# A decoder trunk's output projection, from one product per token tile to Strassen's seven products

## Chip, cores and metric

The kernel is one program on 1 core of a Trainium2 chip. The metric is the device time of one execution in microseconds (us). The engines are named as in the profile: PE (TensorE matmul; PEld is its weight load), DVE (VectorE), ACT (ScalarE), POOL (GpSimd) and SP (SyncE), whose queue SPq issues most DMAs.

## What is computed

One hybrid mixer layer for 2048 prompt tokens and 32 sample tokens (8 x 4). Four channel groups of 512 are made and gated, put side by side to 2048 channels, and projected to 1024 columns:

```python
mix = jnp.concatenate([y_c * jax.nn.silu(cg), y_p * jax.nn.silu(pg),
                       y_s * jax.nn.silu(sg), y_m * jax.nn.silu(mg)], axis=-1)   # conv, pool, attention, memory
out = rms_norm(mix @ w_out, post_g)       # (tokens, 2048) @ (2048, 1024)
return x + out, ...                       # then a final rms_norm over 1024 columns
```

Everything is float32. The change concerns `mix @ w_out` and the work that runs beside it.

## The kernel before

The program has three parts in time. First, up to about 1500 us, the input projection `z` on PE, with the sample group's attention over gathered pages (POOL issues the gathers), the depthwise convolution on DVE and the memory attention woven in. Then the prompt's stick-breaking attention, up to about 1979 us. Last the output projection, with the rest of the conv branch (`conv_post`) woven in. Every finished quarter of `mix` lies in DRAM as `mixd[16, 128, tokens]`: 16 chunks of 128 channels, group g being chunks 4g to 4g+3 (0 conv, 1 pool, 2 attention, 3 memory).

PE's order is the order of the code; the other engines' orders are set by a scheduler when the kernel is built, and each engine then works strictly in that order. `sp.dma_start` and `wq.dma_start` both go to SP's queue, which is in order too. A tile taken from a pool with `bufs=n` waits until the tile n places earlier is no longer read.

A float32 product is made of three matmuls on reduced operands: hi x hi, hi x lo, lo x hi, where hi is a cast to `fp32r` (ACT) and lo the difference (DVE). For the projection, `out_weights` loads a 128 x 512 piece of `w_out` (`wor`) and splits it into `wohi` and `wolo`. `out_mix` loads a part, that is 128 tokens of one group (`mr`, 256 KB in runs of 512 B), and splits it into `mh` (ACT) and `ml` (DVE). `out_part` makes a part's matmuls into the PSUM tile `acc`: 4 channel chunks x 3, each 128 x 512. A token tile has 4 parts in each column half; 16 prompt tiles and a tile of the 32 sample tokens (2 matmuls per chunk) give 1600 matmuls. `order` lists (column half, token tile, group): in half 0 the conv group is taken `LAG` = 5 tiles late, since `conv_post` still makes it. `out_keep` copies half 0 to SBUF, and `out_tile` does both norms and the residual once half 1 is there. `prepare` splits `AHEAD` = 4 parts ahead of PE.

`conv_post` has eight blocks of 256 tokens (the last 288). For each: `cs`, the sum over four channel chunks of `cy`; its mean by a matmul `cm`; centring of `cy`; squares `csq` and their sum; a variance by a matmul `cv`; root and reciprocal `crs`; scale, sigmoid `csg` and split into `shi` and `slo`; then four pointwise products `cz` of 12 matmuls each. Each `cz` is multiplied with a gate loaded into `cgt` and stored to `mixd`. `cgt` has two buffers, which `cs` uses too. `OPACE` sets how many PE steps lie between two steps of `conv_post`.

## Time and profile before

| | us |
|---|---|
| three runs | 2425.78, 2427.82 (median), 2430.87 |
| profiled execution, its own time | 2425.78 |
| its span from first to last instruction | 2424.1 |
| PE, DVE, ACT, POOL busy | 2321.3, 1633.9, 1108.1, 1235.3 |

The profiled execution is the fastest of the three, 2.0 us under the median. Busy times of PE overlap, because a matmul's record lasts longer than the step to the next one; how densely PE works is read from the starts of its matmuls.

### The profile page before, as it was taken

Reading aid. Unit: us, or ns where it says so; the run is one execution under the profiler, and the core shown is the slowest. Engines: PE = TensorE matmul, PEld = TensorE weight load, DVE = VectorE, ACT = ScalarE, POOL = GpSimd, SP = SyncE. Lnnn points to the kernel's source line nnn. Section 1 sums busy time; section 2 is a strip of 40 time slices with the busy share of each in tenths; the row PEclk is TensorE's granted clock in tenths of the full one; section 3 lists DMA queues with packets and bytes.
Section 4 is the critical chain, followed back from the end, with each engine's and each line's share of the span. In section 5 each row is a group of like instructions: output and inputs, shape, how many; then the busy total and the mean of one; then the engine's idle time right before and its main releaser. Section 6 shows DMA issues by size and latency. Waiting matters only on the chain. (4 is left out here: it accounts for less than half of the span.)

```text
span 2424.1 us, 42161 instructions
## 1 busy us (share of the span) xinstructions
PE 2321.3 (96%) x16154; PEld 1806.4 (75%) x16154; DVE 1633.9 (67%) x2268; ACT 1108.1 (46%) x1890; POOL 1235.3 (51%) x1289
## 2 busy tenths in 40 slices
PE   6999999999999899999999998999999989999998
PEld 6998878898888677777777776555555558788786
DVE  5332775959747663577877778788898846565554
ACT  5332353242442222223241434788988955444443
POOL 1554545556474555555556564667776833320222
PEclk9999999999999999999999999999999999999999
DMA  5688988878778899877778767733323125446564
GB/s 184 206 265 293 346 315 288 283 260 281 250 262 302 271 344 326 315 267 274 275 266 275 259 222 188 215 77 112 94 79 92 36 88 146 130 117 190 164 203 132
DMA packets 350931, 526.47 MB, mean 217 GB/s; under 512 B 27585, under 2 KB 252225, under 8 KB 334330
## 3 DMA queue, kind: packets, MB, share of 16 engines
q1 hardware_dynamic: 295354, 255.07, 34.8%
q0 software_dynamic: 55376, 268.72, 31.2%
q8 instruction: 127, 2.08, 0.3%
q14 instruction: 74, 0.61, 0.1%
HBM read 448.31 MB, written 76.00 MB: 216 GB/s over the span
## 5 line engine op out<-in xcount | busy, mean ns | idle before, releaser
L903 DVE STREAM_TRANSPOSE T<-kt 128x1024 f32<-128x1024 f32 x256 | 308.9, 1226 | 192.5 <-PE sSA L916 174.4
L870 POOL DMA_INDIRECT vt<-in_cache_v_dram,idv x256 | 250.7, 979 | 240.4 <-PE sO L955 179.3
L561 DVE SCALAR_TENSOR_TENSOR cacc<-U,par,cacc 128x512 f32<-128x512 f32 x480 | 360.3, 751 | 11.8
L1255 POOL TENSOR_TENSOR be<-be,E 128x512 f32<-128x512 f32 (+2 forms) x320 | 303.3, 955 | 116.9 <-DVE E L1246 50.8
L1246 DVE TENSOR_TENSOR_SCAN E<-gam,cr,ZM 128x513 f32<-128x513 f32 x192 | 233.2, 1265 | 15.6 <-ACT gam L1231 13.7
L870 POOL DMA_INDIRECT kt<-in_cache_k_dram,idk x128 | 125.9, 983 | 204.2 <-DVE T L903 150.3
L1649 PE MATMUL acc<-wohi,mh 128*128 128x512 f32 (+1 forms) x544 | 219.6, 404 | 3.9 <-ACT mh L1479 3.9
L1649 PE MATMUL acc<-wolo,mh 128*128 128x512 f32 (+1 forms) x544 | 213.7, 393 | 0.0
L1266 PEld LDWEIGHTS AT<-ident,be 128*128 128x128 f32 x1088 | 117.8, 142 | 127.7 <-ACT at L1272 44.0
L1649 PE MATMUL acc<-wohi,ml 128*128 128x512 f32 x512 | 202.5, 396 | 1.1 <-DVE ml L1482 1.1
L1231 ACT ACTIVATE gam<-S,nbias_bc 128x1024 f32<-128x1024 f32 (+1 forms) x160 | 172.3, 1077 | 51.5 <-ACT be L1233 19.5
L1226 PE MATMUL S<-kT,Q 128*128 128x512 f32 (+1 forms) x640 | 177.9, 401 | 6.8 <-DMA Q<-qd 2.8
L1266 PE MATMUL AT<-ident,be 128*128 128x128 f32 x1088 | 158.4, 284 | 14.2 <-DVE at L1270 3.9
L1233 ACT ACTIVATE be<-S,bias_bc 128x1024 f32<-128x1024 f32 (+1 forms) x160 | 171.2, 1070 | 0.0
L1282 PE MATMUL av<-at,V 128*64 128x512 f32 (+3 forms) x640 | 153.0, 557 | 1.8 <-DVE sbo L1287 1.8
L916 PE MATMUL sSA<-T,W 128*32 128x128 f32 x4096 | 139.9, 277 | 4.3 <-DVE T L903 3.5
L1479 ACT CAST mh<-mr 128x512 fp32r<-128x512 f32 (+1 forms) x136 | 79.3, 600 | 127.5 <-PE acc L1649 71.0
L916 PEld LDWEIGHTS sSA<-T,W 128*32 128x32 f32 x4096 | 105.0, 110 | 41.8 <-issue 35.5
L1510 POOL TENSOR_TENSOR oxt<-oxt,oy 128x1024 f32<-128x1024 f32 (+1 forms) x16 | 43.6, 2724 | 179.5 <-DVE oy L1505 133.6
L1482 DVE TENSOR_TENSOR ml<-mr,mh 128x512 fp32r<-128x512 f32 x124 | 97.2, 803 | 44.2 <-ACT mh L1479 43.6
L1226 PEld LDWEIGHTS S<-kT,Q 128*128 128x128 f32 x640 | 107.2, 196 | 23.0 <-issue 3.5
L955 PE MATMUL sO<-vt,saT 128*32 128x512 f32 x1024 | 122.4, 592 | 0.0
(561 smaller groups left out, 5959.4 us busy)
## 6 DMA issues: line engine op xcount, KB each, us to landing
mr<-mixd SPq DMA_DIRECT2D x128, 256.0 KB
Q<-qd SPq DMA_DIRECT2D x64, 256.0 KB
xtp<-in_x_prompt_dram SPq DMA_DIRECT2D x16, 512.0 KB
kT<-kd SPq DMA_DIRECT2D x64, 128.0 KB
wor<-in_w_out_dram SPq DMA_DIRECT2D x32, 256.0 KB
oxt<-in_x_prompt_dram SPq DMA_DIRECT2D x16, 512.0 KB
out_dram<-oy SPq DMA_DIRECT2D x15, 512.0 KB
wr0mem<-in_w_mem_kv_dram SPq DMA_DIRECT2D x8, 512.0 KB
```

Source lines behind the costliest of these rows:

```text
L561: dve.scalar_tensor_tensor(out=ps, in0=U[:, a + k : a + k + H], scalar=wd[:, k : k + 1], in1=ps, op0=ALU.mult, op1=ALU.add)
L870: pool.indirect_dma_start(out=dst, out_offset=None, in_=rows, in_offset=bass.IndirectOffsetOnAxis(ap=idx, axis=0))
L903: dve.transpose(T[:, 2 * hh : 2 * hh + 2].rearrange("p s j t -> p (s j t)"), kt[:, 2 * hh : 2 * hh + 2].rearrange("p s j d -> p (s j d)"))
L916: pe.matmul(sSs[n][32 * g : 32 * g + 32, P * ml : P * (ml + 1)], lhsT=W[:, jj, :], rhs=T[:, :, jj, :], start=i == 0, stop=i == 3, tile_pos ...
L1226: pe.matmul(S[:, j, :w], lhsT=Q[hh][:, x, P * (q2 + j) : P * (q2 + j + 1)], rhs=KT[hp, hh, kc][:, :w], start=x == 0, stop=x == 1)
L1231: act.activation(out=ga[:, :, 512 - w : 512], in_=S[:, :, :w], func=AF.Sigmoid, bias=nbias_bc[:, h : h + 1], scale=-1.0)
L1233: act.activation(out=be[:, :, :w], in_=S[:, :, :w], func=AF.Sigmoid, bias=bias_bc[:, h : h + 1])
L1246: dve.tensor_tensor_scan(out=E[:, j][:, ::-1], data0=ga[:, j][:, ::-1], data1=ZM[:, 0:1].to_broadcast([P, 513]), initial=carry[hh, q2][:, ...
L1255: pool.tensor_tensor(out=be[:, j, :m], in0=be[:, j, :m], in1=E[:, j, 513 - w : 513 - w + m], op=ALU.mult)
L1266: pe.transpose(ap_[:, P * qt : P * (qt + 1)], A[hp, qb, kc, hh, qt][:, P * r : P * (r + 1)], ident)
L1282: pe.matmul(av[64 * hh : 64 * hh + 64, c], lhsT=V[:, 4 * kc + r, 64 * hh : 64 * hh + 64], rhs=ats.pop((hp, qb, kc, r, hh))[:, c], start=dg ...
L1649: pe.matmul(o[:rows], lhsT=m[i][:, k, :rows], rhs=W[hf, 4 * g + k][w], start=g == 2 and k == i == w == 0, stop=g == 0 and k == 3 and (i if ...
```

## The change

The 2048 channels are cut into A-columns 1 (groups 2 and 3) and 2 (groups 1 and 0), the tokens into pairs of tiles (i = 0 to 7), and the columns into halves of 512. For each pair the four products of a 2 x 2 block product, eight half-size ones, are replaced with seven (Winograd's form of Strassen's scheme):

- products 1 to 7 of sums of A-blocks (`TERMS`) and of B-blocks (`operand`); a part is now (product, pair, channel half), and its matmuls are as before. `order` runs product 1 for all pairs, then 7, 6, 2, and then 5, 4, 3 pair by pair. The sample tokens (i = `LAST` = 8) use four products and no sums. 1408 matmuls remain.
- the sums of weight blocks are made in the first part by `out_sums`: 4 loads and 4 stores of 512 KB and 8 POOL operations for each of four calls, kept in DRAM as `wsd`. The weights are split once for each product: 56 pieces instead of 32.
- the sums of token blocks are made by `out_combine` (products 7 and 6 on DVE, 2 and 5 on POOL), one operation a part, and those of 7, 6 and 2 are stored to DRAM as `msd` and loaded again by the product that follows on them.
- the seven results are put together by `out_ready`: 8 DVE adds with a PSUM operand per pair, through SBUF arrays `C11`, `U2` and `U3`. The finished first block goes to DRAM (`c11d`) and comes back as `oh`.
- `out_tile` adds the residual in halves on DVE or POOL, and squares in halves.
- in `conv_post` the sums over four chunks, three POOL operations each, become one DVE `TENSOR_REDUCE` each; `csq` is one tile, `csg` has two buffers of its own, and `OPACE` is 0.66.
- `mh` and `ml` have 4 buffers instead of 6, `mr` 7 instead of 4.

```diff
-OPACE = 0.95
+OPACE = 0.66
-LAG = 5
+OH = 2
+OX = 3
+RAWS = 7
...
+    def out_sums(*js):
+        ws = {}
+        for j in js:
+            for n, rows in enumerate(half_rows(j)):
+                ws[j, n] = k4(f"ws{j}_{n}", [P, 2, 512], F32)
+                sp.dma_start(ws[j, n].rearrange("p a c -> p (a c)"), w_out0[rows])
+        for _ in range(5):
+            yield
+        for j in js:
+            (b11, b12), (b21, b22) = [(ws[j, n][:, 0], ws[j, n][:, 1]) for n in range(2)]
+            pool.tensor_tensor(out=b11, in0=b12, in1=b11, op=ALU.subtract)
...
+            wq.dma_start(wsd[j, 0], ws[j, 0])
...
-                sums[i] = channel_sum([ys[i][:, c, :N] for c in range(4)], *[
-                    cp.tile([P, CW], F32, tag="cgt", name=f"cs{n}{a0}", bufs=2)[:, :N] for n in range(2)])
+                sums[i] = cp.tile([P, CW], F32, tag="cgt", name=f"cs{a0}", bufs=2)[:, :N]
+                dve.tensor_reduce(out=sums[i], in_=ys[i][:, :, :N].rearrange("p c t -> p t c"), axis=AX.X, op=ALU.add)
...
-            sqs[i] = channel_sum(sq, sq[0], sq[2])
+            dve.tensor_reduce(out=sqs[i], in_=sq.rearrange("p c t -> p t c"), axis=AX.X, op=ALU.add)
...
+    TERMS = {1: ((0, 0),), 7: ((0, 0), (1, 0)), 6: ((1, 1), 0), 2: ((0, 1), 1), 5: ((1, 0), (1, 1)), 4: ((1, 1),),
+             3: (2,)}
...
+    def out_combine(x):
+        prod, i, h = x
+        if len(raws[x]) == 2:
+            a, b = raws[x]
+            o = a if prod == 5 else b
+            (pool if prod in (2, 5) else dve).tensor_tensor(out=o, in0=a, in1=b, op=ALU.add if prod == 5 else ALU.subtract)
+            if prod != 5:
+                sp.dma_start(msd[(7, 6, 2).index(prod), i, h], o)
...
+        if prod == 1:
+            act.copy(C11[:, i], o)
+        elif prod == 7:
+            dve.tensor_tensor(out=U3[:, i], in0=o, in1=C11[:, i], op=ALU.add)
+        elif prod == 6:
+            dve.tensor_tensor(out=U2[:, i], in0=o, in1=C11[:, i], op=ALU.add)
+            dve.tensor_tensor(out=U3[:, i], in0=o, in1=U3[:, i], op=ALU.add)
+        elif prod == 2:
+            dve.tensor_tensor(out=C11[:, i], in0=o, in1=C11[:, i], op=ALU.add)
+            square(C11[:, i], t, 0)
+            sp.dma_start(c11d[i], C11[:, i])
+        else:
+            if prod == 5:
+                dve.tensor_tensor(out=U2[:, i], in0=o, in1=U2[:, i], op=ALU.add)
+            dve.tensor_tensor(out=o, in0=o, in1=(U2 if prod == 3 else U3)[:, i], op=ALU.add)
+            half = 0 if prod == 4 else 1
+            square(o, t, half)
...
-        if not last:
-            pool.tensor_tensor(out=xt[:rows], in0=xt[:rows], in1=y[:rows], op=ALU.add)
+            (dve if last or n or t % 2 else pool).tensor_tensor(out=xt[:, hs], in0=xt[:, hs], in1=src, op=ALU.add)
+            act.activation(out=junk[:rows], in_=xt[:, hs], func=AF.Square, accum_out=ss[:, n + 1 : n + 2])
...
+    order = [(p, i) for p, n in ((1, 9), (7, 8), (6, 8), (2, 9)) for i in range(n)]
+    order += [(5, 0), (4, 0), (5, 1), (4, 1), (3, 0), (3, 1), (5, 8), (3, 8)]
+    order += [(p, i) for i in range(2, 8) for p in (5, 4, 3)]
```

DVE's order in the second conv block, from its first gate to the next block's centring. Names end in a number of their own; `ml0_6_1` is half 0, tile 6, group 1, and in the changed kernel `mr7_1_1_1` is product 7, pair 1, half 1, operand 1. Before:

```order
L1404 SCALAR_TENSOR_TENSOR cgt256_0_20471<-cz256_0_20473,par_113,cgt256_0_20471 128x256
L1482 TENSOR_TENSOR ml0_1_0_20517<-mr0_1_0_20518,mh0_1_0_20516 128x512
L1482 TENSOR_TENSOR ml0_6_2_20570<-mr0_6_2_20571,mh0_6_2_20569 128x512
L1404 SCALAR_TENSOR_TENSOR cgt256_1_20494<-cz256_1_20496,par_113,cgt256_1_20494 128x256
L1482 TENSOR_TENSOR ml0_6_3_20626<-mr0_6_3_20627,mh0_6_3_20625 128x512
L1489 COPY okeep_19991<-acc0_0_19840 128x512
L1404 SCALAR_TENSOR_TENSOR cgt256_2_20526<-cz256_2_20528,par_113,cgt256_2_20526 128x256
L1404 SCALAR_TENSOR_TENSOR cgt256_3_20549<-cz256_3_20551,par_113,cgt256_3_20549 128x256
L1482 TENSOR_TENSOR ml0_6_1_20661<-mr0_6_1_20662,mh0_6_1_20660 128x512
L1375 RECIPROCAL crs512_20585<-crs512_20585 128x256
L1380 SCALAR_TENSOR_TENSOR cy512_20166<-cy512_20166,par_113,crs512_20585 128x256 x4
```

The same place in the changed kernel:

```order
L1429 SCALAR_TENSOR_TENSOR cgt256_0_20515<-cz256_0_20517,par_116,cgt256_0_20515 128x256
L1531 TENSOR_TENSOR mr7_1_1_1_20697<-mr7_1_1_0_20695,mr7_1_1_1_20697 128x512
L1429 SCALAR_TENSOR_TENSOR cgt256_1_20545<-cz256_1_20547,par_116,cgt256_1_20545 128x256
L1531 TENSOR_TENSOR mr7_2_0_1_20718<-mr7_2_0_0_20716,mr7_2_0_1_20718 128x512
L1429 SCALAR_TENSOR_TENSOR cgt256_2_20568<-cz256_2_20570,par_116,cgt256_2_20568 128x256
L1546 TENSOR_TENSOR ml7_0_0_20670<-mr7_0_0_1_20535,mh7_0_0_20669 128x512
L1429 SCALAR_TENSOR_TENSOR cgt256_3_20588<-cz256_3_20590,par_116,cgt256_3_20588 128x256
L1531 TENSOR_TENSOR mr7_2_1_1_20802<-mr7_2_1_0_20800,mr7_2_1_1_20802 128x512
L1381 TENSOR_REDUCE cs768_20618<-cy768_20444 128x256
L1400 RECIPROCAL crs512_20622<-crs512_20622 128x256
L1389 TENSOR_TENSOR cy768_20444<-cy768_20444,cm768_20676 128x256
```

What moved: the token sums stand between the gates, and the channel sum `cs`, which takes a `cgt` buffer, stands in DVE's queue where POOL's queue had it.

DVE's order in the last stage, between two output tiles. Before (half 1, tiles 8 to 10):

```order
L1499 TENSOR_TENSOR oss7_23113<-oss7_23113,ssk_19992 128x1
L1501 RECIPROCAL oss7_23113<-oss7_23113 128x1
L1505 SCALAR_TENSOR_TENSOR oy7_23112<-okeep_19991,oss7_23113,gpost_22340 128x512
L1505 SCALAR_TENSOR_TENSOR oy7_23112<-acc1_7_23043,oss7_23113,gpost_22340 128x512
L1482 TENSOR_TENSOR ml1_9_1_23182<-mr1_9_1_23183,mh1_9_1_23181 128x512
L1517 RECIPROCAL oss7_23113<-oss7_23113 128x1
L1520 SCALAR_TENSOR_TENSOR oy7_23112<-oxt7_23110,oss7_23113,gfin_22341 128x1024
L1482 TENSOR_TENSOR ml1_9_0_23216<-mr1_9_0_23217,mh1_9_0_23215 128x512
```

In the changed kernel (products 5, 4 and 3 of pairs 3 to 5):

```order
L1611 SCALAR_TENSOR_TENSOR acc3_3_23420<-acc3_3_23420,oss6_23455,gpost_22708 128x512
L1586 TENSOR_TENSOR U2_20067<-acc5_4_23478,U2_20067 128x512
L1612 TENSOR_TENSOR oxt6_23453<-oxt6_23453,acc3_3_23420 128x512
L1587 TENSOR_TENSOR acc5_4_23478<-acc5_4_23478,U3_20068 128x512
L1546 TENSOR_TENSOR ml3_4_1_23539<-mr3_4_1_0_23491,mh3_4_1_23538 128x512
L1614 TENSOR_TENSOR oss6_23455<-oss6_23455 128x1
L1546 TENSOR_TENSOR ml5_5_0_23577<-mr5_5_0_0_23512,mh5_5_0_23576 128x512
L1616 RECIPROCAL oss6_23455<-oss6_23455 128x1
L1619 SCALAR_TENSOR_TENSOR oxt6_23453<-oxt6_23453,oss6_23455,gfin_22709 128x1024
L1587 TENSOR_TENSOR acc4_4_23520<-acc4_4_23520,U3_20068 128x512
```

What moved: the adds of `out_ready` and the residual adds stand between the splits that PE waits for.

SP's queue while half 1 is made before, with one output store for four loads of `mr`:

```order
L1477 DMA mr1_8_1_23094<-mixd_63 128x4x128
L1522 DMA out_0_dram<-oy5_22934 128x1024
L1495 DMA oxt7_23110<-in_x_prompt_dram 128x1024
L1477 DMA mr1_8_0_23128<-mixd_63 128x4x128
L1477 DMA mr1_9_2_23147<-mixd_63 128x4x128
L1477 DMA mr1_9_3_23165<-mixd_63 128x4x128
```

and in the middle of product 2 of the changed kernel:

```order
L1523 DMA mr2_3_1_0_22290<-mixd_63 128x4x128
L1497 DMA wor5_4_22250<-wsd_70 128x512
L1497 DMA wor5_5_22276<-wsd_70 128x512
L1517 DMA mr2_3_1_1_22292<-msd_71 128x512
L1533 DMA msd_71<-mr2_3_0_1_22257 128x512
L1583 DMA c11d_69<-C11_20074 128x512
L1523 DMA mr2_4_0_0_22325<-mixd_63 128x4x128
```

What moved: stores that wait for POOL or DVE (`msd`, `c11d`) stand ahead of loads that PE needs.

## The prediction

> **What bounds the kernel now.** I read the page's busy shares and its chain of waits first:

> ```profile
> PE 2321.3 (96%) x16154; PEld 1806.4 (75%) x16154; DVE 1633.9 (67%) x2268; ACT 1108.1 (46%) x1890; POOL 1235.3 (51%) x1289
> PE acc L1649 13%; PE cz L1401 1%; DMA mixd<-cgt 1%; PE av L1282 0%; PE AT L1266 0%; DMA cgt<-gcd 0%; POOL slo L1386 0%; PE cm L1361 0%; DVE crs L1375 0%; POOL cs L1336 0%; DVE cgt L1404 0%; POOL cs L1335 0%; DVE ml L1482 0%; SPq L1477 0%; PE S L1226 0%
> ```

> PE is the bound, and the chain that ends last runs through the projection's `acc`. Its first stage also has conv links (`cgt`, `slo`, `cm`, `crs`), so two stages must be told apart: the one with the conv blocks and the one behind it. In the chain in order of time and the instructions of `cz`, the blocks and the end stand at:

> ```profile
> L1401 PE MATMUL cz<-shi,pwhi x128: 276/282/416, 2005.0 to 2194.0; 128*128 128x256 f32 x112, 128*128 128x288 f32 x16
> 2184.70 1.59 PE cz L1401 x12
> 2194.55 219.17 PE acc L1649 x955
> ```

> The first of eight blocks starts its products at 2005.0 and the eighth at 2184.7: seven block steps take 179.7 us, 25.7 each. After 2194.55 PE runs 955 `acc` matmuls in one piece, 0.2295 us each. The rate inside a piece, from the timeline (first and last of 94 matmul starts in a row):

> ```profile
> 2299.55 0.39 PE L1649 MATMUL acc<-wohi,mh 128*128 128x512 f32 x1
> 2320.84 0.39 PE L1649 MATMUL acc<-wohi,mh 128*128 128x512 f32 x1
> 2060.28 0.28 PE L1401 MATMUL cz<-shi,pwhi 128*128 128x256 f32 x1
> 2061.59 0.28 PE L1401 MATMUL cz<-shi,pwlo 128*128 128x256 f32 x1
> 2066.71 0.67 PE L1372 MATMUL cv<-csq,ones_ln 128*128 128x256 f32 x2 [0.62 <-DVE cgt L1404]
> ```

> 21.29 us over 93 steps is 0.229 us per `acc` matmul, whatever its record's 0.39; 12 `cz` starts give 1.31 over 11, 0.119; a `cv` or `cm` takes 0.7. Busy time by stage (us, then PE, PEld, DVE, ACT, POOL, clock, DMA share, GB/s):

> ```profile
> 2005.00:2185.00 180.00, 171.28 (x882) 144.35 (x883) 108.70 (x176) 85.98 (x176) 62.40 (x71) 0.98 0.45 127
> 2185.00:2414.00 229.00, 228.71 (x1016) 184.43 (x1014) 119.35 (x205) 95.90 (x208) 43.62 (x17) 1.00 0.60 180
> ```

> DVE has 71 us to spare in the first of these, 110 in the second.

> **The change, part by part.** *Fewer matmuls.* 1600 become 1408: 192 x 0.229 = 44.0 us, the most PE alone could give. By PE's order both kernels have 114 `acc` matmuls ahead of the first block's `cz`; in the seven block steps there are 516 before and 355 now, behind them 970 and 939. So 161 matmuls (36.9 us) go from the conv stage and only 31 (7.1 us) from the long piece. In the conv stage PE now needs 355 x 0.229 + 336 x 0.119 + 13 x 0.7 = 130 us, 18.6 per block.

> *The conv stage on DVE.* These rows are the means of that stage, then those of the last stage, the PSUM-reading add (32 partitions of the same 512 columns), and the only transposed reduce over four chunks:

> ```profile
> L1482 DVE TENSOR_TENSOR ml<-mr,mh 128x512 fp32r<-128x512 f32 x47 | 42.2, 921 | 18.7 <-ACT mh L1479 18.6
> L1380 DVE SCALAR_TENSOR_TENSOR cy<-cy,par,crs 128x256 f32<-128x256 f32 (+1 forms) x28 | 15.1, 599 | 0.1
> L1384 DVE SCALAR_TENSOR_TENSOR cy<-cy,par,csg 128x256 f32<-128x256 f32 (+1 forms) x30 | 14.6, 540 | 4.9 <-ACT csg L1383 4.9
> L1375 DVE RECIPROCAL crs<-crs 128x256 f32<-128x256 f32 (+1 forms) x7 | 12.4, 1777 | 2.8 <-ACT crs L1374 2.8
> L1364 DVE TENSOR_TENSOR cy<-cy,cm 128x256 f32<-128x256 f32 (+1 forms) x27 | 10.2, 416 | 0.4 <-PE cm L1361 0.4
> L1404 DVE SCALAR_TENSOR_TENSOR cgt<-cz,par,cgt 128x256 f32<-128x256 f32 x28 | 13.5, 483 | 39.2 <-DMA cgt<-gcd 24.0 <-PE cz L1401 10.3 <-PE acc L1649 3.2
> L1463 DVE TENSOR_TENSOR wolo<-wor,wohi 128x512 fp32r<-128x512 f32 x11 | 7.4, 690 | 2.2 <-ACT wohi L1462 1.4 <-DMA mixd<-cgt 0.7
> L1482 DVE TENSOR_TENSOR ml<-mr,mh 128x512 fp32r<-128x512 f32 x55 | 39.9, 748 | 11.9 <-ACT mh L1479 11.7
> L1520 DVE SCALAR_TENSOR_TENSOR oy<-oxt,oss,gfin 128x1024 f32<-128x1024 f32 x14 | 18.0, 1285 | 1.5
> L1505 DVE SCALAR_TENSOR_TENSOR oy<-okeep,oss,gpost 128x512 f32<-128x512 f32 x15 | 11.3, 752 | 0.5
> L1517 DVE RECIPROCAL oss<-oss 128x1 f32<-128x1 f32 x14 | 2.3, 164 | 49.9 <-ACT oss L1516 49.9
> L1657 DVE TENSOR_TENSOR both<-both,acc x2: 669/672/676, 2231.2 to 2272.6; 32x512 f32<-32x512 f32 x2
> L1155 DVE TENSOR_REDUCE smR<-smOm 128x128 f32<-128x512 f32 x2 | 2.1, 1057 | 0.0
> ```

> The reduce has 128 outputs of four; the new ones have 256, so I take 2.1 us each (bounds: 1.06, the same row if its length did not count, and 2.5). DVE's order holds, in the seven block steps, 28 gates x 0.483 + 28 x 0.599 + 28 x 0.540 + 7 x 1.777 + 24 x 0.416 = 67.8 of conv as before; 12 reduces x 2.1 = 25.2, new; 28 splits x 0.75 and two small = 21.6 (0.75 as behind the conv stage, since most of POOL's sums that lengthened 0.75 to 0.92 are gone); 25 token sums x 0.75 = 18.8, new; 16 weight splits x 0.69 = 11.0; 12 PSUM adds x 0.67 = 8.1, and one both-add 0.7. Sum 153 us, 21.9 per block: more than PE's 130. So DVE, not PE, paces this stage: `ml` and the token sums that PE needs stand behind the conv work in its queue, and so each wait there counts. Before, the waits there were 24.0 us on gates from DMA, 18.6 on `mh`, 10.3 on `cz`, about 5 on `csg`. Those on `cz` and most on `mh` fall away when PE is ahead; the gates' round trip (store, then load into the same buffer) is partly covered by the token sums that now stand between; new on DVE is the wait of `cs` for a `cgt` buffer, which POOL had:

> ```profile
> POOL cs L1334 <- DMA mixd<-cgt: 53.2, 5, 12.1
> SPq L1396 <- DMA mixd<-cgt: 35.2, 19, 4.6
> ```

> Part of POOL's 53.2 was idleness anyway; on DVE it can cost 0 to 3 us a block. I take 2.0 us of waits a block in all (bounds 0.5 and 6; before it was over 7, with DVE half idle): 153 + 14 = 167 us against 179.7, so **-13 us** (bounds -37, PE's pace with the loss of before, below, and +15). The first block's start stays: DVE is idle until attention ends in both, 0 (-1 to +4).

> *Behind the conv stage.* PE gives **-7**. Against it: in the last stage a pair of tiles costs DVE 6 splits x 0.75 + 4 PSUM adds x 0.67 + 4 x 0.75 + 3 adds x 0.75 + 2 x 1.285 + 8 small x 0.16 = 16.3 us, and PE 72 x 0.229 = 16.5. The 110 us of slack are gone; a wait of half a us a pair shows, and the splits stand behind `oxt` loads and ACT's roots in the same queue: before, DVE waited 49.9 us for 14 such roots, 3.6 each, free in its slack. Where other work now stands between add and root, most of that is filled. I take +0.5 us a pair, **+4** (0 to +16).
> In product 2 each part moves `mr` and `msd` in, `msd` out, and its share of `c11d` and weights: 0.79 + 0.13 + 0.23 = 1.15 MB in 12 x 0.229 = 2.74 us.

> ```profile
> q1 hardware_dynamic: 33250, 28.79, 59.6%
> L1477 SPq DMA_DIRECT2D mr<-mixd x136: 359/377/1333, 1877.9 to 2391.0; - x136
> ```

> The first row is of 2245 to 2405 us: 28.79 MB took 59.6% of 160 us, 302 GB/s if always busy. At that rate a part needs 3.8 us, 16 parts +17; if c11d and weights can run late, 2.6, nothing. I take **+5** (0 to +17), nearer the second, since those weights are first used a product later. [...] SP issues 168 more DMAs x 0.38 us, 64 us of 460 that are mostly idle; that loads wait behind stores is in the waits above.

> *First part.* 32 POOL adds and 16.8 MB of DMA.

> ```profile
> 600.00:1500.00 900.00, 880.46 (x6859) 683.58 (x6852) 623.14 (x823) 292.51 (x526) 497.69 (x460) 1.00 0.80 273
> L676 POOL TENSOR_TENSOR U<-U,sg1cb 128x512 f32<-128x512 f32 x8 | 8.8, 1103 | 0.9 <-ACT sg1cb L674 0.8
> ```

> 32 x 1.1 = 35 us on a POOL with 400 us free, 56 us of DMA where 180 are free; both covered by `z` on PE. But POOL's page gathers queue behind adds that wait for their load, and PE waits for pages: **+2** (-1 to +8). ACT gains 24 casts and 8 copies at about 0.6, 19 us, with half its time free: 0. The tail gains a PSUM add and an output chain just ahead of it on DVE: **+1** (0 to +3).

> *Sum.* -13 - 7 + 4 + 5 + 2 + 1 = -8 on the profiled execution's 2425.8 (span 2424.1, 1.7 around it): **2418 us**, 0.4% under the median 2427.8, which is 2.0 above that execution. A difference under 0.2% (4.9 us) this kernel's measurement can't tell from none.

> **Rivals.** *DVE's queue makes the conv stage longer (slower).* Place: `cgt` and `cs` in DVE's order, each waiting for a store. It decides at (179.7 - 153) / 7 = 3.8 us of waits a block; with 6 us the stage takes 195, +15, and with the other terms +5 the time is 2446. For it: before, DVE waited over 7 us a block, and DMA was at 0.45 there where the changed kernel doubles its loads. Against: half of those waits were on PE.
> *The gain is given back behind the conv stage (no change).* DVE at 16.3 of 16.5 and DMA near its rate: both at half their upper bounds, +16 instead of +9, give 2425.
> *PE stays the bound (much faster).* If reduces and waits are short, the conv stage falls to PE's 130 plus what it lost before, 179.7 - (516 x 0.229 + 40 + 9.1) = 13, so 143, and behind it little is lost: 2425.8 - 37 - 7 + 5 = 2387. Against: DVE's 153.
> [...]
> That the change isn't made is excluded: 1408 matmuls stand in PE's order.

> **Chances and range.** Forecast, 2406 to 2422: 0.38, the reduce at its short bound within it. PE's pace, 2380 to 2405: 0.12. No change: 0.20. Slower, mostly by DVE's queue: 0.30. So faster 0.50, same 0.20, slower 0.30. The range 2393 to 2446 cuts half of PE's case and the longest waits; the likeliest case alone has 2406 to 2422.

> **What would show it.** Right: `acc` x1408; conv steps of 23 to 24.5 us with DVE over 85% busy; a long piece near 0.229 us a matmul; new reduces of 2 us. Wrong: DVE waits of over 4 us a block on `mixd<-cgt`, PE waits on `ml` of over 10 us behind the conv stage, a DMA share over 0.9 in product 2, or a first part that ends later than at 1513 us, where the first `E` starts:

> ```profile
> L1246 DVE TENSOR_TENSOR_SCAN E<-gam,cr,ZM x192: 1229/1262/1284, 1513.0 to 1954.5; 128x513 f32<-128x513 f32 x192
> ```

## The result, and the profile after

The changed kernel takes 2461.93 us in the median of 4 runs (2459.88 to 2464.02), the kernel before beside it 2429.35 (4 runs, 2425.78 to 2431.51): a ratio of 1.0136 (95% interval 1.0118 to 1.0153). It is 1.4% slower. The forecast was 2418 us, with a range of 2393 to 2446.

The page of the kernel after, its busy shares and the chain that ended last:

```profile
PE 2309.7 (94%) x15962; PEld 1785.2 (73%) x15962; DVE 1738.5 (71%) x2414; ACT 1121.9 (46%) x1939; POOL 1254.6 (51%) x1297
PE acc L1755 2%; DMA mr<-msd 1%; DVE ml L1546 1%; DMA wor<-wsd 1%; PE cz L1426 1%; DMA mixd<-cgt 1%; DMA mr<-mixd 0%; ACT junk L1613 0%; DVE oxt L1619 0%; DVE wolo L1505 0%; POOL mr L1531 0%; ACT junk L1551 0%; DMA cgt<-gcd 0%; POOL oxt L16
```

The products' matmuls have the names `acc`, at L1755 now, and there are 1408 of them. Before, they made 13% of the chain; now 2%, and loads, splits and casts stand in their place. PE is busy for only 11.6 us less, although 44 us of matmuls are gone. The stages tell why. Busy time in four windows, which end at the first scan `E`, the first `cz`, the eighth block's first `cz` and the last `acc`; the columns after the window are its length, then PE, PEld, DVE, ACT and POOL busy, PE's granted clock, DMA share and GB/s. The kernel before:

```profile
0.00:1513.00 1513.00, 1460.24 (x11692) 1207.80 (x11692) 1001.14 (x1371) 515.37 (x956) 803.07 (x773) 0.99 0.80 272
1513.00:2005.00 492.00, 461.10 (x2567) 269.86 (x2567) 399.99 (x509) 408.47 (x544) 326.20 (x430) 0.98 0.36 101
2005.00:2184.50 179.50, 170.78 (x878) 143.89 (x879) 108.20 (x176) 85.76 (x175) 61.90 (x71) 0.98 0.45 127
2184.50:2413.70 229.20, 229.20 (x1019) 184.89 (x1018) 119.85 (x205) 95.86 (x209) 44.12 (x17) 1.00 0.60 180
```

The kernel after, in the same stages:

```profile
0.00:1529.90 1529.90, 1468.41 (x11692) 1213.16 (x11692) 1005.00 (x1371) 515.91 (x956) 844.76 (x805) 0.99 0.82 280
1529.90:2013.90 484.00, 456.17 (x2566) 266.32 (x2566) 403.00 (x511) 409.59 (x549) 320.90 (x421) 0.99 0.38 104
2013.90:2191.70 177.80, 149.39 (x718) 121.08 (x718) 136.73 (x213) 81.74 (x156) 26.36 (x29) 0.90 0.67 201
2191.70:2441.30 249.60, 235.70 (x987) 184.64 (x987) 184.04 (x301) 109.81 (x265) 62.53 (x44) 0.96 0.81 252
```

Adding what follows the last `acc` (10.4 us before, 16.5 after), the 33.7 us between the two spans are: first part +16.9, attention and the lead of the projection -8.0, the seven steps of the conv stage -1.7, behind them +20.4, the tail +6.1.

The third rows are the heart of it. PE's need there fell by 37 us and the stage stayed as long. Its idle time is length minus busy time: 8.7 us before, 28.4 after. And the granted clock was 0.98 before and 0.90 after, so a tenth of 177.8, 17.8 us, was lost with PE busy. Take both away: 179.5 - 8.7 - 3.6 = 167.2 and 177.8 - 28.4 - 17.8 = 131.6. That is what the matmuls there need by the prediction's rates, 167 and 130. Nearly all of the 37 us came back: 19.7 as waits and 14.2 as slow clock.

What PE waited for in the seven steps before (us in total, times, longest):

```profile
PE cm L1361 <- POOL cs L1336: 5.8, 3, 2.5
PE cz L1401 <- ACT shi L1385: 2.3, 1, 2.3
PE cv L1372 <- DVE cgt L1404: 1.3, 2, 0.7
PE cz L1401 <- DVE cgt L1404: 0.8, 1, 0.8
PE cz L1401 <- POOL slo L1386: 0.7, 2, 0.5
```

And after:

```profile
PE cm L1386 <- DVE cs L1381: 13.5, 6, 3.4
PE cz L1426 <- POOL slo L1411: 7.9, 14, 2.4
PE cz L1426 <- ACT shi L1410: 5.7, 7, 1.8
PE cv L1397 <- DVE cgt L1429: 2.2, 2, 1.5
```

All four of the second list are links of the conv blocks: the channel sum `cs`, its mean on PE (`cm`), the variance (`cv`), root, scalings, sigmoid, the halves `shi` and `slo`, the products `cz`, the gates `cgt`, and then the next block's `cs`. Not one wait is for the projection's splits.

How a wait is paid twice, from PE's timeline after (start, duration; idle time before it in brackets):

```profile
2158.53 0.39 PE L1755 MATMUL acc<-wolo,mh 128*128 128x512 f32 x1
2158.76 0.40 PE L1755 MATMUL acc<-wohi,ml 128*128 128x512 f32 x1
2162.53 0.81 PE L1386 MATMUL cm<-cs,ones_ln 128*128 128x288 f32 x2 [3.38 <-DVE cs L1381]
2163.56 0.63 PE L1755 MATMUL acc<-wolo,mh 128*128 128x512 f32 x1
2163.99 0.63 PE L1755 MATMUL acc<-wohi,ml 128*128 128x512 f32 x1
...
2166.77 0.40 PE L1755 MATMUL acc<-wohi,mh 128*128 128x512 f32 x1
2167.00 0.39 PE L1755 MATMUL acc<-wolo,mh 128*128 128x512 f32 x1
```

Ahead of the wait of 3.38 us the starts are 0.23 us apart, behind it 0.43, and from 2166.77 on 0.23 again: for about 3.4 us PE works at half speed (the granted clock is 0.60 over the 4.3 us from 2162.5 to 2166.8, that is half for 3.4 of them).

### The profile page after: what moved, and what is told of

Same layout as the page of the kernel before. It is cut to its first block, busy times and chain, and to the rows that moved or that the text cites. A ratio compares the mean times of both kernels' runs of the same rounds, so it can differ in the third digit from the quotient of the medians.

```text
span 2457.8 us, 42287 instructions
## 1 busy us (share of the span) xinstructions
PE 2309.7 (94%) x15962; PEld 1785.2 (73%) x15962; DVE 1738.5 (71%) x2414; ACT 1121.9 (46%) x1939; POOL 1254.6 (51%) x1297
## 5 line engine op out<-in xcount | busy, mean ns | idle before, releaser
L1278 DVE TENSOR_TENSOR_SCAN E<-gam,cr,ZM 128x513 f32<-128x513 f32 x192 | 232.9, 1263 | 14.4 <-ACT gam L1263 13.1
L1755 PE MATMUL acc<-wohi,mh 128*128 128x512 f32 (+1 forms) x480 | 199.2, 415 | 8.1 <-ACT mh L1543 8.0
L1263 ACT ACTIVATE gam<-S,nbias_bc 128x1024 f32<-128x1024 f32 (+1 forms) x160 | 172.6, 1078 | 51.0 <-issue 20.7
L1755 PE MATMUL acc<-wolo,mh 128*128 128x512 f32 (+1 forms) x480 | 194.5, 405 | 0.0
L1755 PE MATMUL acc<-wohi,ml 128*128 128x512 f32 x448 | 182.2, 407 | 5.7 <-DVE ml L1546 5.7
L948 PE MATMUL sSA<-T,W 128*32 128x128 f32 x4096 | 141.3, 278 | 11.4 <-DVE T L935 10.2
L1531 POOL TENSOR_TENSOR mr<-mr,mr 128x512 f32<-128x512 f32 x32 | 48.0, 1499 | 149.2 <-DMA mr<-mixd 65.6
L1411 POOL TENSOR_TENSOR slo<-cy,shi 128x256 fp32r<-128x256 f32 (+1 forms) x32 | 30.6, 976 | 170.0 <-ACT shi L1410 152.2
L1304 ACT COPY at<-AT 128x512 f32<-128x512 f32 x192 | 109.0, 656 | 18.0 <-PE AT L1298 18.0
```

The source lines that it names most:

```text
L948: pe.matmul(sSs[n][32 * g : 32 * g + 32, P * ml : P * (ml + 1)], lhsT=W[:, jj, :], rhs=T[:, :, jj, :], start=i == 0, stop=i == 3, tile_pos ...
L1263: act.activation(out=ga[:, :, 512 - w : 512], in_=S[:, :, :w], func=AF.Sigmoid, bias=nbias_bc[:, h : h + 1], scale=-1.0)
L1278: dve.tensor_tensor_scan(out=E[:, j][:, ::-1], data0=ga[:, j][:, ::-1], data1=ZM[:, 0:1].to_broadcast([P, 513]), initial=carry[hh, q2][:, ...
L1755: pe.matmul(o[:rows], lhsT=m[a][:, k, :rows], rhs=W[prod, 4 * h + k][w], start=not cont and h == k == n == 0, stop=h == 1 and k == 3 and n ...
```

## Experiments

Sixteen kernels were run. They ran on several chips, on which the kernel before took 2424.05 to 2429.35 us, so kernels are compared by their ratios to the kernel before on the same chip, given with 95% intervals. "Steps" are the seven block steps of the conv stage, in the profiled execution. In the recorded expectations, "chain theory" says that the delays of a conv block's links, one behind the other, set the steps, and "queue theory" that DVE's amount of work does. Some kernels have a name, in brackets behind the heading, which later runs use.

**1. The sums of weight quarters alone, in the kernel before** (sums_only).

```
+        yield from z_groups(0, GROUPS[0][14:27])
+        tasks.add(out_sums(0, 1))
...
+            tasks.add(out_sums(2 * n + 2, 2 * n + 3))
```

> The kernel before with the sixteen loads, 32 POOL adds and sixteen stores of the weight sums put into its first part as in the changed kernel; nothing reads the sums. If the sums cost the first part its time, the first 513-wide scan E starts 8 to 16 us later than before's 1513.0 and the run takes 2437 to 2445. If the 16 us seen between the two profiles are one execution's own (6 to 7 us of them stand there before the first of these loads is issued at 526 us), the run takes 2429 to 2435.

Measured: 2433.79 us in 10 runs, ratio 1.003 (1.0014 to 1.0046): 7 us, between 3 and 11. The first `E` of this kernel, and that of the changed one:

```profile
L1274 DVE TENSOR_TENSOR_SCAN E<-gam,cr,ZM x192: 1229/1262/1287, 1519.3 to 1960.5; 128x513 f32<-128x513 f32 x192
```
```profile
L1278 DVE TENSOR_TENSOR_SCAN E<-gam,cr,ZM x192: 1228/1258/1283, 1529.9 to 1970.4; 128x513 f32<-128x513 f32 x192
```

6.3 us later than before, against 16.9 in the changed kernel, whose first part is the same. The time lies in the second expectation's range and the first scan comes earlier than the first expectation had it; but by the interval the sums are not free. So the sums cost about 7 us, and the rest of the 16.9 is taken as this execution's own. In the profiles of all 16 kernels with the sums the first `E` starts between 1514.5 and 1529.9, at 1521.9 in the mean; in the two without, at 1512.4 and 1513.0.

**2. Work taken off DVE: splits and token sums of products 1, 7 and 6 on POOL.**

```
-        for d, f in (..., (0, lambda x: out_split(x, dve))):
+        for d, f in (..., (0, lambda x: out_split(x, pool if x[0] in (1, 7, 6) else dve))):
...
-    (pool if prod in (2, 5) else dve).tensor_tensor(out=o, in0=a, in1=b, op=...)
+    pool.tensor_tensor(out=o, in0=a, in1=b, op=...)
```

> The changed kernel with the mix splits (ml) and token sums (mr) of products 1, 7 and 6 on POOL instead of DVE: some 55 operations of 0.75 us, 40 us of DVE's 142 us, leave the conv stage. If DVE's queue paces that stage, the seven block steps fall from 183 to about 150 us and the run takes 2425 to 2435. If the steps are set by the chain of hops of a conv block (cv, root, reciprocal, scale, sigmoid, shi, slo, cz) with too few matmuls of the projection to cover it, they fall by 0 to 12 us and the run takes 2450 to 2462.

Measured: 2474.33 us, ratio 1.019 (1.0168 to 1.0212), slower than the change itself and outside both expectations. The steps, and PE's waits in them:

```profile
2009.90:2198.50 188.60, 152.43 (x717) 123.72 (x717) 119.09 (x160) 82.55 (x157) 97.12 (x87) 0.89 0.68 203
PE cz L1426 <- POOL slo L1411: 14.6, 14, 3.8
PE cz L1426 <- ACT shi L1410: 12.3, 6, 4.9
PE cm L1386 <- DVE cs L1381: 8.6, 6, 2.7
```

DVE had 17.6 us less to do and the steps grew by 10.8. The wait for `cs` shrank by 5 us, those for `slo` and `shi` grew by 13: `slo` now stands among splits and sums in POOL's queue, 58 operations more with 70.8 us more of busy time, about 1.2 us each. So DVE's amount of work doesn't set the steps, and it points to the delay of single links.

**3. The channel sums back on POOL** (three additions in place of a reduce, as in the kernel before).

```
-                dve.tensor_reduce(out=sums[i], in_=ys[i]..., axis=AX.X, op=ALU.add)
+                sums[i] = channel_sum([ys[i][:, c, :N] for c in range(4)], ...)
```

> The changed kernel with the two channel sums of each conv block back on POOL, three additions each, as before; the 14 reduces of 2 us leave DVE. Chain theory: the sum's link is as long on POOL as on DVE (three adds of 0.6 to 1 us), so the steps stay at 172 to 184 us and the run at 2456 to 2466. Queue theory: DVE's 137 us in the stage fall to 110, the steps fall by 15 to 25 us, and the run takes 2438 to 2448.

Measured: 2458.51 us, ratio 1.0155 (1.0115 to 1.0196). The steps took 181.2 us, as the chain theory has it; PE waited 22.4 us for `cs` instead of 13.5. The reduce that the change brought to DVE is not the cause, and as a link it is the shorter of the two.

**4. More projection matmuls between the conv blocks.**

```
-OPACE = 0.66
+OPACE = 0.80
```

> The changed kernel with 0.80 instead of 0.66 for the number of projection steps per conv step: about 63 instead of 52 projection matmuls stand between two conv blocks, 70 more in the seven block steps. If the chain of hops sets the step, the added matmuls fill idle time of PE, the steps stay at 183 us (within 8) and the run gets 10 to 18 us faster than the changed kernel, 2444 to 2452, with fewer stretches at half clock. If DVE's queue sets it, each added part brings a split and a token sum, the steps grow by about 9 us, and the run is at 2455 to 2465.

Measured: 2459.88 us, ratio 1.0137 (1.0101 to 1.0173), the change's own. The steps hold 63 matmuls more (14.4 us) and took 188.0 us, 10 more: the numbers of the queue theory, and a miss of the chain theory. PE's idle time stayed at 29.9 us; the clock rose to 0.95. Taken with runs 2 and 3, where less work on DVE made the steps no shorter, a possible reading is that more cover brings more splits and sums into the queues in which the links stand, so that the chain grows with its cover. No run shows that by itself.

**5. One link taken out: the first channel sum ahead of the products of two blocks earlier** (early_cs).

```
-                sums[i] = cp.tile([P, CW], F32, tag="cgt", name=f"cs{a0}", bufs=2)[:, :N]
+                sums[i] = cp.tile([P, 4, CW], F32, tag="csq", name=f"cs{a0}", bufs=1)[:, 0, :N]
...
-            yield from point(i)
             total(i + 2)
+            yield from point(i)
```

> The changed kernel with the first channel sum of a conv block (cs, a reduce of 2 us on DVE) put ahead of the products of two blocks earlier, into a buffer of its own instead of one of the gates'. Chain theory: PE's 13.5 us of waits of cm for cs in the conv stage go, and with them about five of the eight stretches at half clock, so the seven block steps fall from 178 to 155 to 165 us and the run takes 2440 to 2452. Queue theory (DVE's amount of work sets the step): DVE has as much to do as before, the steps stay within 5 us and the run at 2456 to 2466.

The buffer that `cs` gets here is that of `csq`. Measured: 2449.96 us, ratio 1.0108 (1.0091 to 1.0125). The time is inside the chain theory's range, but partly by the chip, on which the kernel before took 2424.05; and the steps fell only to 172.6 us, where 155 to 165 was expected. PE's waits in them:

```profile
PE cz L1426 <- POOL slo L1411: 12.4, 17, 2.6
PE cz L1426 <- ACT shi L1410: 8.9, 11, 2.4
PE cv L1397 <- DVE cgt L1429: 0.6, 1, 0.6
```

The wait for `cs` is gone altogether, and the next link of the chain took 8 of its 13.5 us.

**6. The chain taken apart: variance, root, scalings and sigmoid ahead as well** (early_scale).

```
             total(i + 2)
+            if i + 1 < len(blocks):
+                scale(i + 1)
             yield from point(i)
             if i + 1 < len(blocks):
-                scale(i + 1)
+                halve(i + 1)
```

`scale` ends with the sigmoid's product now; `halve` has what followed it, `shi`, `slo` and the next block's load.

> As early_cs, and the variance product, root, reciprocal, both scalings and the sigmoid of a block also stand ahead of the products of the block before it, so that only the casts shi and the differences slo lie between two blocks' products. Chain theory: PE's 13.6 us of waits for shi and slo go as well, the steps fall to 140 to 155 us, near the 130 that PE needs, and the run takes 2430 to 2442. Queue theory: 175 to 185 us and 2456 to 2466, perhaps more because the gates now queue behind the scalings.

Measured: 2423.89 us in 10 runs, ratio 1.0002 (0.999 to 1.0015): the run is as fast as the kernel before. The steps are in the chain theory's range; the time is 6 us under it, on a chip on which the kernel before takes 2424.05. The steps, and what PE waits for in them:

```profile
2004.80:2152.30 147.50, 133.48 (x717) 113.44 (x716) 134.58 (x208) 77.15 (x150) 27.27 (x29) 0.97 0.77 231
PE cv L1397 <- DVE cq L1392: 15.1, 6, 4.7
PE cz L1431 <- DVE cgt L1434: 2.2, 2, 2.0
```

Same matmuls, about the same work on DVE (134.6 us), same engines, another order (and `csq`'s buffer for `cs`): 30.3 us less. So in the conv stage the place of the links in the order had held PE.

**7. PE kept busy in its waits**, with matmuls whose result is overwritten.

```
+            for _ in range(14 * (i > 0)):
+                pe.matmul(mps[:, :CB], lhsT=cw[0][:, 0, :P], rhs=cw[0][:, 1, :CB], start=True, stop=True)
             pe.matmul(mps[:, :N], lhsT=ones_ln, rhs=sums.pop(i), start=True, stop=True)
...
+                for _ in range(4 * (not co)):
+                    pe.matmul(ps[:, :CB], lhsT=whi[:, 0, :P], rhs=whi[:, 1, :CB], start=True, stop=True)
```

> The changed kernel with matmuls on PE, in the places where it waits in the conv stage, whose result is overwritten: 14 of 128x256 ahead of each cm and 4 ahead of the first cz of a block, 2.1 us a block where PE waits 3.8. If half clock costs time by itself, the eight stretches (34 us) in the conv stage fall below 15 us, and the seven steps from 178 to 165 to 172: 2448 to 2456. If the chain of hops sets the steps whatever PE's clock is, they stay at 174 to 182 and the run at 2456 to 2465; if the added matmuls come later than the waits, 2462 to 2470.

```profile
2006.20:2179.20 173.00, 155.44 (x830) 128.75 (x829) 135.26 (x210) 79.47 (x153) 24.77 (x28) 0.97 0.68 202
```

Measured: 2453.32 us, ratio 1.0099 (1.0079 to 1.0119). The steps came between the two expectations. With 15 us of useless matmuls (18 a block at 0.119) they are 4.8 us shorter, with a clock of 0.97 instead of 0.90 and 17.6 us of idle time instead of 28.4. So it points to half clock costing time by itself, beyond the chain; how much of the 17.8 us would be saved by that alone stays open, since the added matmuls fill waits as well.

**8. Bytes taken out of product 2** (p2_single). Product 2 multiplies its first load; the difference with the second is made there for product 3. Here that difference is left out, and product 3 takes the stored operand of product 6 in its place.

```
-    ... 2: ((0, 1), 1), ... 3: (2,)}
+    ... 2: ((0, 1),), ... 3: (1,)}
```

> The changed kernel with product 2 (and product 3, which reads what product 2 stored) taking one operand where it should take the difference of two: 16 loads, 16 POOL subtractions and 16 stores of 256 KB are left out, 8.4 MB in the 57 us of product 2, so its output is not the reference's. If the traffic (or SP's queue with it) sets product 2's pace, its eight pairs fall from 57 us towards PE's 44 and the run takes 2446 to 2453. If the weights of product 5 alone hold it up, the pairs stay at 52 to 57 us and the run at 2455 to 2464.

Measured: 2441.77 us, ratio 1.0084 (1.0067 to 1.01), that is 13 us less than the change's 1.0136. The eight pairs of product 2 in the changed kernel, and then here, each from product 6's last PSUM addition to product 2's last:

```profile
2232.50:2289.60 57.10, 50.24 (x192) 37.64 (x191) 27.06 (x39) 20.41 (x42) 18.82 (x12) 0.91 0.85 265
```
```profile
2221.20:2265.40 44.20, 44.20 (x192) 35.31 (x191) 24.52 (x40) 21.44 (x44) 3.95 (x3) 1.00 0.71 214
```

PE runs without a gap, at the 44 us that 192 matmuls need. So these loads and stores, with the subtraction, had held it: 13 us.

**9. Which part of it: POOL's subtraction, loads one by one, or the bytes?** All but one of these kernels stand on top of early_scale. The subtraction on DVE (es_dve2):

```
-            (pool if prod in (2, 5) else dve).tensor_tensor(...)
+            (pool if prod == 5 else dve).tensor_tensor(...)
```

> The kernel early_scale (2424 us, eight pairs of product 2 in 56 us) with product 2's subtraction on DVE (0.73 us) instead of POOL (1.3 to 1.8 us). If the subtraction's link is what holds product 2 (the load behind it in SP's queue waits for the store that waits for it), its pairs fall from 56 to 46 to 50 us and the run takes 2414 to 2420. If the amount of traffic or the number of raw buffers in flight holds it, the pairs stay at 53 to 57 us and the run at 2421 to 2427.

Measured: 2425.81 us, ratio 0.9996 (0.9979 to 1.0013). Its eight pairs took 47.7 us instead of 55.7, as the link's case has it, but product 6's last two pairs took 14.0 instead of 10.3, and product 5's first addition came 16.7 us behind product 2's last instead of 13.4. So 1 us of the three remains, and the run is no faster. More loads in flight, the weights' earlier (es_loads):

```
+WRAWS = 5
+RAW2 = 4
...
+                raws[j] = (tmp or opm).tile([P, 512], F32, tag="wraw" if tmp else "raw", ..., bufs=WRAWS if tmp else 2)
...
+                r = tmp.tile([P, 512], F32, tag="raw2", ..., bufs=RAW2)
```

> The kernel early_scale with more loads in flight around product 2, in the space that the conv pool leaves: four more buffers for its second operands, five instead of two for the raw weights of products 5 and 4, product 5's first loads ahead of product 2, product 4's in its second half; amount of traffic and engine work unchanged. If loads one by one behind each other in SP's queue hold product 2, its pairs fall from 56 to 45 to 50 us, and product 5 starts 2 to 4 us sooner: 2411 to 2417. If the amount of traffic holds it (0.85 of the DMA time), the pairs stay at 52 us or more and the run at 2418 to 2426.

Measured: 2425.51 us, ratio 0.9998 (0.9984 to 1.0011). `wraw` holds the weights of products 5 and 4, `raw2` product 2's second operand. Product 2's pairs took 47.5 us, but the pair ahead of it took 12.1 instead of 7.7: about half of the wait moved to where the loads had gone. The run is no faster. Of that, the weights' buffers alone, on the change itself (`wor` with `bufs=5`, `op2` opened ahead of product 5's weights; deep_weights):

> The changed kernel with five buffers instead of two for the raw quarters of the weights of products 5, 4 and 3 (in the space that the conv pool leaves, opened before product 5's weights instead of after them). If the time lost between 2240 and 2300 us comes from those loads waiting one by one for a buffer in SP's queue with all later loads behind them, 8 to 12 us come back: 2450 to 2454. If it comes from the traffic itself (DMA busy 0.86 there) it stays at 2458 to 2464.

Measured: 2460.11 us, ratio 1.0132 (1.0111 to 1.0154), by its time the case of the traffic; in the profiled execution the pairs took 51.6 us instead of 57.1, and the last stage 3 us more. Last, the bytes moved to the last stage, with a correct difference for product 3, made on POOL (es_redo3):

```
-    ... 2: ((0, 1), 1), ... 3: (2,)}
+    ... 2: ((0, 1),), ... 3: ((0, 1), 1)}
```

> The kernel early_scale, with the difference that product 3 needs made in product 3 from two loads, instead of in product 2, where it is made beside the product, stored, and loaded again: in product 2 16 loads, 16 POOL subtractions and 16 stores of 256 KB go (8.4 MB of 15), in the last stage 16 loads (4.2 MB) and 16 POOL subtractions come. Nothing is left out. If the bytes hold product 2, its pairs fall from 56 us to 44 to 47 and the last stage, with DMA at 0.77, takes 0 to 4 us more: 2409 to 2417, faster than the kernel before. If the gain is given back in the last stage, where loads then come from POOL's queue later: 2419 to 2426.

```profile
2202.40:2246.60 44.20, 44.20 (x191) 35.37 (x190) 23.94 (x39) 21.32 (x44) 4.37 (x3) 1.00 0.71 212
```

Product 2 is at PE's pace again, with nothing left out. From product 6's first addition to product 5's first, early_scale takes 119.0 us, es_dve2 118.1, es_loads 115.6 and this kernel 107.0. So the engine of the subtraction and the number of buffers are the smaller part. But loads, stores and subtractions left product 2 together here, so that the bytes among them had held it is likely, not shown.

But the run is no faster than early_scale: 2428.66 us in 12 runs, ratio 0.9998 (0.9984 to 1.0011). Behind the conv stage only 6.5 us are saved in the profiled execution (243.7 against 250.2). The rest was given back in the last stage, the second case of the expectation. The additions of products 5, 4 and 3 in early_scale, and then here:

```profile
L1595 DVE TENSOR_TENSOR acc<-acc,U x24: 668/692/696, 2261.2 to 2405.9; 128x512 f32<-128x512 f32 x24
```
```profile
L1595 DVE TENSOR_TENSOR acc<-acc,U x24: 680/691/700, 2263.5 to 2413.9; 128x512 f32<-128x512 f32 x24
```

From the first to the last of them it takes 150.4 us instead of 144.7, and the first comes 16.9 us behind product 2's last addition instead of 13.4: 9 of the 11.5 us that product 2's pairs had saved. The steps were also 2.7 us longer in that execution, and its first part was one of the late ones. With the edits of es_loads and es_redo3 together:

> As es_redo3, with the loads of es_loads: deeper buffers for the weights of products 5 and 4 and product 5's loads ahead of product 2. If bytes and not single loads set the pace, it is within 4 us of es_redo3; if product 5's start (4 us late) still hangs on loads one by one, 2 to 4 us faster than it.

Measured: 2429.77 us, ratio 1.0001 (0.999 to 1.0013), as the first of its cases has it.

**10. DVE's share of the last stage,** on top of es_loads (es_loads_split4).

```
-        for d, f in (..., (0, lambda x: out_split(x, dve))):
+        for d, f in (..., (0, lambda x: out_split(x, pool if x[0] == 4 else dve))):
```

> As es_loads, and product 4's splits (ml, two for each pair of tiles) on POOL instead of DVE in the last stage, where DVE is busy 87% of the time and PE runs 18.3 us a pair of token blocks for 16.5 of matmuls. If DVE's work paces the last stage, 1.5 us a pair come back: 5 to 9 us under es_loads. If PE waits there for loads or for single late splits, POOL's split of 1.3 us, a link longer, makes it the same or up to 6 us slower.

Measured: 2429.45 us, ratio 1.0015 (1.0 to 1.003), 4 us more than es_loads. It points to loads or single late splits, not DVE's sum of work, as what PE waits for there too; which of the two stays open.

**11. The same order in the kernel before, and the pace again.** First run 6's order in the kernel before (before_early). Its two partial sums take buffers of `csq`, and `scale` stands ahead of the channel sum here, not behind it:

```
+            if i + 1 < len(blocks):
+                scale(i + 1)
+            total(i + 2)
             yield from point(i)
-            total(i + 2)
             if i + 1 < len(blocks):
-                scale(i + 1)
+                halve(i + 1)
```

> The kernel before with early_scale's order of a conv block: channel sum, variance, root, scalings and sigmoid ahead of the products of the block before. Its seven steps take 179.6 us with 167.5 of matmuls, so at most 12 us can come back. If PE's work sets the step there, as the sums say, 5 to 11 us: 0.9955 to 0.998 of before. If the gates, now queued behind the scalings, hold PE, no change or slower.

Measured: 2428.75 us, ratio 1.0014 (1.0002 to 1.0026). The steps fell to 170.8 us, but the first block's products start 10.7 us later, after one wait of 11.7 us for a `cs`: no gain in all, where 5 to 11 us were expected if PE's work set the step. So this kind of order is worth 30 us in the steps to the changed kernel and 9 to the one before, in which PE idled for 8.7 us only.

Then the pace in es_redo3 (es_pace75):

```
-OPACE = 0.66
+OPACE = 0.75
```

> The kernel es_redo3 (seven steps of 150 us, of which PE idles 14 and loses 8 to half clock) with 0.75 instead of 0.66 for the pace: some 49 more projection matmuls, 11 us, in the seven steps, as many fewer behind. If PE's idle time now takes them, the steps grow by 2 to 5 us and the run gets 5 to 8 us faster than es_redo3, 0.9965 to 0.998 of before. If DVE (137 us busy of 150) sets the step, they grow by 8 to 12 us and the run stays at 0.999 to 1.001.

```profile
2009.70:2167.80 158.10, 145.41 (x766) 122.56 (x765) 144.38 (x228) 82.45 (x157) 30.52 (x29) 0.97 0.80 240
```

Measured: 2425.02 us, ratio 1.0002 (0.999 to 1.0013); the steps grew by 8 us for 11 us of matmuls. DVE is busy for 144.4 of 158.1 here and for 134.6 of 147.5 in early_scale, 91% in both. That fits DVE as the next limit, as the expectation's second case says. But early_scale's longest waits are still for one DVE link (`cv` for `cq`, 15.1 us), and no run takes work off DVE in this order, so it isn't shown. No version was found that is faster than the kernel before.

## Why the prediction was wrong

The forecast and the measured differences of the two profiled executions, stage by stage (us):

| | forecast | measured |
|---|---|---|
| first part | +2 | +16.9 (7 by the runs of sums_only) |
| up to the first block's products | 0 | -8.0 |
| seven steps of the conv stage | -13 | -1.7 |
| behind the conv stage | -7 + 5 + 4 = +2 | +20.4 |
| tail | +1 | +6.1 |
| sum | -8 | +33.7 |

Two steps of the prediction failed. In the conv stage the mechanism was wrong. Behind it the mechanisms named were there, but their terms were too small, by 18 us.

*Fewer matmuls: right.* 192 fewer, 161 of them in the conv stage; with the rates used, that stage's sum closes to 1.6 us.

*The conv stage: the first step that failed.* It said "DVE, not PE, paces this stage" and took DVE's work plus 2 us of waits a block. DVE's work was overstated: 153 us against 136.7 measured. Most of that is the way of adding: the rows after sum to 148.0, but the records of neighbouring instructions overlap, and busy time counts the overlap once (before, 114.3 and 108.2). DVE's idle time was understated: 41 us, 5.9 a block, where 2 was taken. But neither is the mechanism: less work on DVE made the steps no shorter (runs 2 and 3), and as much work in another order made them 30 us shorter (run 6). What sets the step is a chain through PE, DVE, ACT and POOL and back. With 74 projection matmuls between two blocks it left PE idle for 8.7 us in the seven steps, with 51 for 28.4; how many would cover it stays open, since 60 (run 4) left as much idle time. A sum over the busiest engine can't see such a chain, and "Those on `cz` and most on `mh` fall away when PE is ahead" looked at DVE's waits, not at PE's. With the chain taken apart the steps are the matmuls' 130 us, 14 of idle time and 4.4 of slow clock, 148.

*The clock: not priced by itself.* Half speed cost 17.8 us in the steps (granted clock 0.90) and 10 behind them (0.96). Behind the wait of 3.38 us about 3.4 us of work were slow; other waits ahead of slow work are shorter, 2.51 us in the last section.

*The reduce: right.* 2.1 us was taken, from the row of half the length:

```profile
L1392 DVE TENSOR_REDUCE cq<-csq 128x256 f32<-128x1024 f32 x6 | 11.8, 1970 | 0.0
L1381 DVE TENSOR_REDUCE cs<-cy 128x256 f32<-128x1024 f32 x5 | 9.4, 1889 | 0.4 <-DMA mixd<-cgt 0.3
```

They took 1.89 to 1.97 us. The forecast's 2406 has the reduce at its short bound of 1.06 us, an estimate from the row of half the length; no run shows it.

*Product 2's DMA: the second step that failed, +5 taken, +12.9 measured* (57.1 against 44.2). Product 5's start, 13.6 us from product 2's last addition where 16 and 24 matmuls need 9.2, adds 4.4. The working had the +17 of a stage held by its bytes, and I took a value near the low end because the weights could run late. Run 8 shows that the loads, stores and subtractions held PE all the same. The rate was 265 GB/s, under the 302 of the estimate (28.79 MB in 59.6% of 160 us, in the kernel before). PE lost the 12.9 us at a DMA share of 0.85, so the sign "over 0.9" was set too high here.

*The last stage: +4 taken, about +8 measured.* From product 5's first addition to the last of all:

```profile
L1587 DVE TENSOR_TENSOR acc<-acc,U x24: 668/691/699, 2303.2 to 2444.8; 128x512 f32<-128x512 f32 x24
```

141.6 us for 584 matmuls that need 133.7. The whole stretch behind the conv stage lost 27.5 us, the 20.4 and the 7.1 of matmuls saved. Idle time (13.9) and slow clock (10.0) make 23.9 of it; the other 3.6 I can't place.

*The first part: +2 taken (-1 to +8), 7 measured by sums_only* (3 to 11), near its bound.

*The tail: +1 taken (0 to +3), +6.1 measured.* The last lines of the chain after:

```profile
2438.82 1.28 DVE oxt L1619
2440.11 0.62 DVE acc L1587
2440.81 0.70 ACT junk L1551 x2
...
2449.01 0.75 DVE acc L1611
```

Two tiles' output chains end 5.5 us of matmuls apart and share DVE and ACT; the last one queues behind the other.

*The first block's start: 0 taken, -8.0 measured* (492.0 to 484.0); all kernels made from the changed one have 484 to 490 there, sums_only has 492. The cause is open.

Of the rivals, the slower one had the sign of the run and DVE's idle time, 6 us a block, but not the mechanism: `cs` waited for a store for 0.3 us in all, and the stage took 177.8 us, not its 195. That the time came nearest to its 2446 is luck, since the loss lay in the first part, behind the conv stage and in the tail.

## What to carry over

Where an engine's cover for a chain of small steps is removed, price the chain first: write down the loop from one block's product to the next, link by link, and compare it with what remains between two blocks. Another order of its links was worth 30 us here, where 37 us of matmuls saved in that stage had brought 1.7. A stage that trades matmuls for stored sums must be checked for its bytes per unit of PE time. And an idle PE paid with its clock as well (0.90 in the steps where it idled for 28.4 us, 0.98 where for 8.7): length = matmuls + idle time + half of the time at half clock closed the conv stage to 2 us before, after and in early_scale.

## What the hardware showed

```profile
2072.39 0.70 PE L1361 MATMUL cm<-cs,ones_ln 128*128 128x256 f32 x2 [1.53 <-POOL cs L1336]
2100.36 0.70 PE L1361 MATMUL cm<-cs,ones_ln 128*128 128x256 f32 x2 [1.74 <-POOL cs L1336]
2150.73 1.33 PE L1361 MATMUL cm<-cs,ones_ln 128*128 128x288 f32 x2 [2.51 <-POOL cs L1336]
```
```profile
2070.00:2080.00 10.00, 8.47 (x37) 6.61 (x36) 8.35 (x16) 6.41 (x16) 3.90 (x5) 1.00 0.30 84
2098.00:2108.00 10.00, 8.26 (x36) 6.49 (x35) 8.87 (x17) 8.05 (x18) 6.43 (x8) 1.00 0.19 54
2150.00:2160.00 10.00, 9.27 (x34) 7.44 (x35) 8.12 (x16) 7.32 (x17) 6.38 (x8) 0.83 0.18 52
```

1.53 and 1.74 us cost nothing beyond themselves, 2.51 us brought a clock of 0.83 over 10 us, that is 1.7 us more. In the changed kernel eight stretches at half clock stand in the seven steps, 34.1 us together. Not all of them follow one long wait: one begins at about 2098, behind four waits of 0.22 to 0.54 us between 2094.6 and 2097.9.

The end of the first part differed by up to 15 us (1514.5 to 1529.9) between 16 profiles, taken on several chips, of kernels whose code for that part is the same. That is more than most terms of this sum: two single profiles can't price 5 us there.
